# Interleaving the high and low parts of every second unit's stationary operand in a decoder step

## The chip, the cores and the metric

The kernel runs on one core of one Trainium2 chip. The metric is device microseconds of one execution. Shown are three runs, of which the median counts, and one more execution that was profiled.

## The reference

The reference is one step of a one-layer decoder: a prompt of 2048 tokens and 32 sample tokens share the weights. After the mixer come cross-attention and a gated feed-forward block, with a norm around each. Nearly all of the arithmetic is in products of activations and weights:

```
m = concat(o_gla, y) @ w_out            # h = x + norm(m)
a = softmax((hn @ w_xq) . mk) . mv @ w_xo   # h = h + norm(a)
f = (silu(hf @ w_gate) * (hf @ w_up)) @ w_down   # h = h + norm(f)
```

All inputs are float32, and the model width is 1024, the hidden width 2816.

## The kernel before, in words

The mixer comes first (to about 850 us). The rest is one long list of passes, each a set of matrix products, and this list is what the change touches. The passes are o (output projection of the mixer), s (scores of the cross-attention), v (its values), g0, g1, g2 (gate and up projections of three blocks of tokens) and d0, d1, d2 (three parts of the sum of the down projection, over 3, 4 and 4 units of the hidden width).

A pass is worked unit by unit. In o, s, v and d a unit is one of 8 groups `j` of 256 tokens; in g it is one of 11 slices `u` of the hidden width, once for the gate and once for the up projection (`m`), so 22 units. Within a unit a block product of 2 by 2 is formed with seven products in place of eight, which `TURN` lists; the sums and differences of blocks that this takes are made on DVE (line 1650). The seven are called parts here. A part is `nt` tiles of 128 rows (3 in d0, 4 elsewhere), and each tile is three matmuls.

Three, because each float32 operand is split into a high part, rounded to the matmul's float32r, and a low part, the rest. `three` (lines 133 to 137) adds high by high, high by low, low by high: lines 135 and 136 load the high stationary part, 137 the low one. The moving operand (tiles `r` and `e`, with 512, 384 or 272 columns) is held through the pass. The stationary operand, 128 by 128 at a time, comes from the tile `s` of class `Unit`: 1024 words on each partition, 4 buffers. `Unit.hi` copies the block as float32r into `s` on ACT (line 1668), and the function that it returns puts the block minus that copy into `s` on DVE (line 1670). The high words lie in words 0 to 511 and the low ones in 512 to 1023, each tile's 128 columns next to each other. Both are made four parts ahead of the matmuls that use them (`ahead_ = 4`); the load of the next raw units is issued with part 6. The matmuls accumulate in four PSUM banks (`accA` twice, `accB`, `accC`), which ACT and DVE empty after each part.

The order of the work is written out by hand: the list `order`, and what is done between parts (pieces of the moving operand, evacuations, sample tokens, norms of finished rows), is recorded in program order on every engine.

Of the kernel before, what the change touches and what calls it, by code (L numbers as in the profile page):

```python
# [20 lines left out]
P = 128  # L21
# [16 lines left out]
def f(ap):  # L38
    return ap.bitcast(F32)
# [3 lines left out]
def hymba_kernel(ctx: ExitStack, tc: tile.TileContext, a: dict, o: dict, dbg: dict | None = None):  # L43
# [49 lines left out]
    mixT = tc.dram_tile([NJ, P, 2048], F32, name="mixT")  # L93
# [39 lines left out]
    def three(ps, wh, wl, ah, al, start, stop, more=False):  # L133

        nc.tensor.matmul(ps, lhsT=wh, rhs=ah, start=start, stop=False, skip_group_check=more)  # L135
        nc.tensor.matmul(ps, lhsT=wh, rhs=al, start=False, stop=False, skip_group_check=more)  # L136
        nc.tensor.matmul(ps, lhsT=wl, rhs=ah, start=False, stop=stop, skip_group_check=more)  # L137
# [1394 lines left out]
    xq = tc.dram_tile([NJ, P, 2048], F32, name="xq")  # L1532
    pT = tc.dram_tile([NJ, P, 2048], F32, name="pT")
# [103 lines left out]
    class Unit:  # L1637

        def __init__(self, src, n):
            self.w = n * P
            self.q = src(praw.tile([P, 2048], F32, name="raw", bufs=2))
            self.t, self.got = {}, {}

# [6 lines left out]
        def hi(self, i):  # L1652

            if i == 1:
                self.op("S1", 2, 3, ALU.add)
            if i == 3:
                self.op("S2", "S1", 0, ALU.subtract)
            if i == 2:
                self.op("S4", 1, "S2", ALU.subtract)
            if i == 5:  # L1660
                self.op("S3", 0, 2, ALU.subtract)
            v = {0: self.q[0], 1: self.q[1], 6: self.q[3]}
            v = v[i] if i in v else self.t[{3: "S1", 2: "S2", 5: "S4", 4: "S3"}[i]]
            w = self.w
            s = pf.tile([P, 1024], F32R, name="s", bufs=4)
            hi, lo = s[:, 0:w], s[:, 512:512 + w]
            h3, l3 = (x.rearrange("p (k c) -> p k c", c=P) for x in (hi, lo))
            nc.scalar.activation(h3, v, AF.Copy)  # L1668
            self.got[i] = hi, lo
            return lambda: nc.vector.tensor_tensor(l3, v, f(h3), op=ALU.subtract)  # L1670

    def unit_x(src, j):

        def load(raw):
            nc.sync.dma_start(out=raw, in_=src[j])
            v = raw.rearrange("p (h u e t) -> p h u e t", h=2, e=2, t=P)
            return [v[:, i // 2, :, i % 2] for i in range(4)]
        return Unit(load, 4)

    def unit_g(u, m):  # L1680
        def load(raw):
            nc.sync.dma_start(out=raw, in_=a["w_gu"][m, u].rearrange("p q c -> p (q c)"))
            return [raw[:, i * 512:(i + 1) * 512].rearrange("p (k c) -> p k c", c=P) for i in range(4)]
        return Unit(load, 4)

    def unit_d(p, j):
        u0, n = PARTS[p]

        def load(raw):
            r = raw[:, 0:n * 512]  # L1690
            nc.sync.dma_start(out=r, in_=aT[j][:, u0:u0 + n].rearrange("p u c -> p (u c)"))
            v = r.rearrange("p (u e h t) -> p u e h t", e=2, h=2, t=P)
            return [v[:, :, i % 2, i // 2] for i in range(4)]
        return Unit(load, n)

# [441 lines left out]
    units = {}  # L2139

    def load_unit(n):
        if n < len(work):
            k, g, _ = work[n]
            kind, i, _ = passes[k]
            units[n] = unit_g(*g) if kind == "g" else unit_d(i, g) if kind == "d" else unit_x({"o": mixT, "s": xq, "v": pT}[kind], g)

    def enter(k):

        nonlocal pg, pd
        kind, i, _ = passes[k]  # L2150
        rate[:] = RATES[kind]
        if kind == "o":
            gain_row(px, "ln_mix_post")
            for u in range(4):
                aux.append(weight_sums(lambda n, u=u: flat2(wqk)[n, u], wX[1], u))
        if kind == "s":
            for u in range(4):
                aux.append(weight_sums(lambda n, u=u: flat2(wvo)[n, u], wX[2], u))
        if kind == "v":
            gain_row(px, "ln_xa_post")  # L2160
        if kind == "g":
            if i == 0:
                rctx.close()
                pg = fctx.enter_context(tc.tile_pool(name="pg", bufs=1, reuse_waits="tile"))

                pg.tile([P, 1536], F32, name="og")
            for u in range(NU):
                if u % (len(BLOCKS) - 1) == i:
                    aux.append(weight_sums(lambda n, u=u: a["w_down"][n, u], wT, u))
            if i + 1 == len(BLOCKS):  # L2170
                aux.append(samples_down())
        if kind == "d" and i == 0:
            fctx.close()
            pd = ctx.enter_context(tc.tile_pool(name="pd", bufs=1, reuse_waits="tile"))
            pd.tile([P, D], F32, name="m")
            pd.tile([P, D], F32, name="ga")
# [40 lines left out]
    lo = [None]  # L2217
# [46 lines left out]
    evs, banks, held, ys = {}, {}, {}, {}  # L2264
# [7 lines left out]
    for e, (n, i) in enumerate(order):  # L2272
        k, g, left = work[n]
        kind, b, gs = passes[k]
        if i == 0:
            cur = n
            if begins[n]:
                if coming:
                    now, coming = coming, None
                enter(k)  # L2280
            held[n] = now
            w = now.w
            if kind == "g":
                if g[1] == 0:
                    sg = {}
                evs[n] = evac_gate(sg, w) if g[1] == 0 else evac_up(sg, w, b, g[0])
            elif kind == "d":
                h = {}
                if n + 1 == len(work):
                    for m in range(2):  # L2290
                        h[m] = stage()
                        nc.sync.dma_start(out=h[m], in_=hX[rows(g, m)])
                top = n in ys
                y = ys.pop(n, {})
                stays = left == 1 and b + 1 < len(PARTS)
                if stays:
                    ys[n + 1] = y
                evs[n] = evac_d(b, g, y, h, top, stays)
            else:
                evs[n] = quads(g, *{"o": (after_mix, True), "s": (after_scores, False), "v": (after_values, True)}[kind])  # L2300
            if left == 2 and k + 1 < len(passes):
                before_loads(k)
                coming = pieces_of(k + 1)
        if i == 2 and n + 1 < len(work) and on_top(n + 1):

            ys[n + 1] = {}
            for m in range(2):
                ys[n + 1][m] = pd.tile([P, D], F32, name="y", bufs=6)
                nc.sync.dma_start(out=ys[n + 1][m], in_=yp[work[n + 1][1]][:, m * D:(m + 1) * D])

        nt = PARTS[b][1] if kind == "d" else 4
        w = held[n].w
        if i == 0:
            banks[n, "A"] = accA.tile([P, 512], F32, name="accA")
        if i == 1:
            banks[n, "B"] = accB.tile([P, 512], F32, name="accB")
        if i == 3:
            banks[n, "C"] = accC.tile([P, 512], F32, name="accC")
        ps = banks[n, {1: "B", 3: "C", 5: "C"}.get(i, "A")]
        while i not in held[n].full:  # L2320
            held[n].step()
        sh, sl = units[n].got[i]
        start = i in (0, 1, 3)
        for kt in range(nt):
            ks = slice(kt * P, (kt + 1) * P)
            three(ps[:, 0:w], sh[:, ks], sl[:, ks], *held[n].moving(i, kt), start and kt == 0, kt == nt - 1, not start)
        if left == 1:
            spent.add((k, i))
        evs[n](NAMES[i], ps)

        todo, later[:] = list(later), []
        for fn in todo:
            fn()
        part(e + ahead_)

        p = coming if work[cur][2] == 1 else now if begins[cur] else None
        if p:
            p.larger()
        tick()
        if p:  # L2340
            p.smaller()
        if kind == "d" or not coming and now.done() and (k != XG or samp2):
            due[1] += rate[1]
            while due[1] >= 10:
                due[1] -= 10
                step(aux)
        pin()
        due[0] += rate[0]
        while due[0] >= 10:
            due[0] -= 10  # L2350
            step(back)
        pin(True)
        if samp2 is None and k == XG and not posts:
            leave_attention()
# [99 lines left out]
```

## Time and profile before

| what | value |
|---|---|
| median of 3 runs | 2815.03 us (2814.23 to 2822.64) |
| the profiled execution | 2820.75 us |
| its span, first to last instruction | 2819.0 us |
| PE busy / weight loads busy | 97% / 84% |
| DVE / ACT / POOL busy | 74% / 52% / 19% |
| matmuls in all / in the nine passes | 15207 / 9408 |
| start of pass o, end of pass d2 | 850.8 us, 2809.0 us |

In the profile PE is the matmul and PEld the weight load, which runs while the matmul before it streams. A matmul's own duration contains its way through the array, and several are under way at once, so the time that a matmul costs is read from the distance between starts, not from its duration. The same holds for weight loads.

### The profile page before, as it was taken

To read this page: it belongs to the slowest core of one execution; us is meant where nothing else is said; L and a number is where in the kernel's file an instruction comes from. 1 tells how busy PE (TensorE), PEld (TensorE's weight loads), DVE (VectorE), ACT (ScalarE), POOL (GpSimd) and SP (SyncE) were. 2 spreads that over 40 slices of the span, in tenths; PEclk is the share of its full clock that TensorE was granted. 3 is DMA by queue.
4 is the path that set the end of the run, shared out by engine and by line. 5 is a ranking of instruction groups with operands and counts; after the bars stand their busy time and mean duration, and the time that the engine had idled before them with its cause. 6 is when DMAs were issued, how large, how long until landed. Compare 5 with 4: busy or idle time off the path is not lost.

```text
span 2819.0 us, 41809 instructions
## 1 busy us (share of the span) xinstructions
PE 2729.5 (97%) x15207; PEld 2367.6 (84%) x15207; DVE 2079.1 (74%) x3831; ACT 1472.8 (52%) x2921; POOL 536.8 (19%) x722
## 2 busy tenths in 40 slices
PE   8999999999998999999899999999999999999998
PEld 8987888788886878878799888899998998788786
DVE  7676677776757787677888787667678878574776
ACT  5545554554546787777755434434445555353432
POOL 2142332321321321015321210001000001000011
PEclk9999999999999999999999999999999999999999
DMA  7345435343266785468864567775234436464765
GB/s 255 113 142 188 148 106 160 118 131 90 83 215 226 282 291 223 146 189 254 263 222 179 177 237 243 253 254 178 98 137 171 156 120 209 168 219 99 239 152 132
DMA packets 151102, 512.17 MB, mean 182 GB/s; under 512 B 18176, under 2 KB 29488, under 8 KB 137328
## 3 DMA queue, kind: packets, MB, share of 16 engines
q1 hardware_dynamic: 94560, 331.81, 36.0%
q0 software_dynamic: 44240, 152.82, 16.8%
q10 hardware_dynamic: 12096, 24.86, 2.7%
q8 instruction: 120, 1.97, 0.3%
q14 instruction: 86, 0.70, 0.1%
HBM read 365.76 MB, written 143.67 MB: 181 GB/s over the span
## 4 chain that ended last, share of the span: by engine, by line
PE 75%; DVE 13%; ACT 5%; DMA 3%; issue 3%; POOL 1%; DVEq 0%; ACTq 0%; SPq 0%; POOLq 0%
PE accA L135 9%; PE accA L136 9%; PE accA L137 9%; PE accC L135 5%; PE accC L136 5%; PE accC L137 5%; PE acc L135 5%; PE acc L136 5%; PE acc L137 5%; PE accB L135 2%; PE accB L137 2%; PE accB L136 2%; DVE s L1670 2%; DVE sum L1650 2%; ACT r L1739 1%
## 5 line engine op out<-in xcount | busy, mean ns | idle before, releaser
L135 PE MATMUL accA<-r,s 128*128 128x512 f32 (+2 forms) x1792 | 637.2, 356 | 19.0 <-ACT r L1739 7.2
L137 PE MATMUL accA<-r,s 128*128 128x512 f32 (+2 forms) x1792 | 629.1, 351 | 2.9 <-DVE s L1670 2.8
L136 PE MATMUL accA<-r,s 128*128 128x384 f32 (+2 forms) x1472 | 502.7, 342 | 2.4 <-DVE r L1743 2.4
L135 PEld LDWEIGHTS accA<-r,s 128*128 128x128 f32 x1792 | 339.2, 189 | 70.9 <-ACT r L1739 11.0
L1668 ACT ACTIVATE s<-sum 128x512 fp32r<-128x512 f32 (+1 forms) x456 | 282.5, 620 | 218.9 <-DVE sum L1650 105.0
L137 PEld LDWEIGHTS accA<-r,s 128*128 128x128 f32 x1792 | 339.7, 190 | 33.2 <-DVE s L1670 4.0
L135 PE MATMUL accC<-r,s 128*128 128x512 f32 (+2 forms) x896 | 318.8, 356 | 9.2 <-ACT s L1668 3.2
L1670 DVE TENSOR_TENSOR s<-sum,s 128x512 fp32r<-128x512 f32 (+1 forms) x456 | 306.8, 679 | 20.1 <-ACT s L1668 19.8
L137 PE MATMUL accC<-r,s 128*128 128x512 f32 (+2 forms) x896 | 314.3, 351 | 0.0
L136 PEld LDWEIGHTS accA<-r,s 128*128 128x128 f32 x1472 | 279.0, 190 | 19.2 <-DVE r L1743 3.6
L1670 DVE TENSOR_TENSOR s<-raw,s 128x512 fp32r<-128x512 f32 (+1 forms) x342 | 233.7, 683 | 52.0 <-ACT s L1668 50.9
L136 PE MATMUL accC<-r,s 128*128 128x384 f32 (+2 forms) x736 | 251.3, 341 | 0.5 <-DVE r L1743 0.5
L1668 ACT ACTIVATE s<-raw 128x512 fp32r<-128x512 f32 (+1 forms) x342 | 213.3, 624 | 72.1 <-PE accC L137 49.8
L129 ACT ACTIVATE whi<-wraw 128x1024 fp32r<-128x1024 f32 (+2 forms) x140 | 128.9, 934 | 184.2 <-PE acc L136 104.5
L135 PEld LDWEIGHTS accC<-r,s 128*128 128x128 f32 x896 | 169.8, 189 | 37.2 <-ACT s L1668 7.8
L130 DVE TENSOR_TENSOR wlo<-wraw,whi 128x1024 fp32r<-128x1024 f32 (+2 forms) x140 | 156.2, 1127 | 48.0 <-ACT whi L129 47.3
L137 PEld LDWEIGHTS accC<-r,s 128*128 128x128 f32 x896 | 169.7, 189 | 14.9 <-DVE s L1670 0.2
L143 POOL TENSOR_TENSOR rs<-ms,nhalf 128x1 f32<-128x1 f32 (+4 forms) x125 | 111.0, 889 | 360.3 <-DVE ms L141 343.9
L135 PE MATMUL acc<-xhl,whi 128*128 128x512 f32 (+1 forms) x464 | 168.1, 363 | 8.3 <-ACT xhl L294 8.2
L137 PE MATMUL acc<-xhl,wlo 128*128 128x512 f32 (+1 forms) x464 | 164.3, 355 | 1.7 <-DVE wlo L130 1.7
L136 PE MATMUL acc<-xhl,whi 128*128 128x512 f32 (+1 forms) x464 | 164.1, 355 | 0.2 <-DVE xhl L295 0.2
L1650 DVE TENSOR_TENSOR sum<-raw 128x512 f32<-128x512 f32 (+1 forms) x228 | 156.4, 686 | 3.6
(696 smaller groups left out, 5857.9 us busy)
## 6 DMA issues: line engine op xcount, KB each, us to landing
raw<-in_w_gu_dram SPq DMA_DIRECT2D x66, 1024.0 KB, 4.9
wraw<-in_w_in_fm_dram SPq DMA_DIRECT2D x52, 512.0 KB, 3.6
wraw<-in_w_in_tm_dram SPq DMA_DIRECT2D x48, 512.0 KB, 3.9
st<-in_w_down_dram SPq DMA_DIRECT2D x37, 512.0 KB, 6.2
aT<-og POOLq DMA_DIRECT2D x22, 768.0 KB, 4.6
raw<-aT SPq DMA_DIRECT2D x16, 1024.0 KB, 6.3
out_y_dram<-y POOLq DMA_DIRECT2D x28, 512.0 KB, 6.1
yp<-y POOLq DMA_DIRECT2D x28, 512.0 KB, 6.6
```

What stands on the lines that cost most here:

```text
L129: last[0] = nc.scalar.activation(hi[:, cs], raw[:, cs], AF.Copy)
L130: nc.vector.tensor_tensor(lo[:, cs], raw[:, cs], f(hi)[:, cs], op=ALU.subtract)
L135: nc.tensor.matmul(ps, lhsT=wh, rhs=ah, start=start, stop=False, skip_group_check=more)
L136: nc.tensor.matmul(ps, lhsT=wh, rhs=al, start=False, stop=False, skip_group_check=more)
L137: nc.tensor.matmul(ps, lhsT=wl, rhs=ah, start=False, stop=stop, skip_group_check=more)
L143: nc.gpsimd.tensor_tensor(out=rs[:rows, :cols], in0=ms[:rows, :cols], in1=nhalf[:rows, :cols], op=ALU.pow)
L1650: nc.vector.tensor_tensor(t[out], x, y, op=o)
L1668: nc.scalar.activation(h3, v, AF.Copy)
L1670: return lambda: nc.vector.tensor_tensor(l3, v, f(h3), op=ALU.subtract)
L1739: nc.scalar.activation(hi, v, AF.Copy)
```

## The change

The stationary tile `s` keeps its size and its four buffers. What changes is where the words lie in it.

- In every odd unit (odd `j`, or odd `u`) the high and low words are interleaved. At a step of 2, which passes o, v, g0, g2 and d1 take, the high word of a column lies beside its low word, and columns are two words apart. At a step of 8, which s, g1 and d2 take, the eight words of one column (four tiles, high and low) lie side by side, and the columns of a tile are eight words (32 bytes) apart. Even units stay as they were.
- In d0, which has 384 words of each part, both parts stay contiguous and begin 16 words (64 bytes) later for each `j`.

So 224 of the 798 splits write at a step of 2 and 126 at a step of 8, and of the 9408 matmuls of the passes 2688 and 1512 load such weights (a third of each in every line of `three`). The arithmetic, the number of instructions, their order on every engine and their waits stay the same; the lines of `Unit.hi` become 1672 (ACT) and 1674 (DVE). The core of the diff:

```
-        def __init__(self, src, n):
-            self.w = n * P
+        def __init__(self, src, n, turn=1, shift=0):
+            self.w, self.turn, self.shift = n * P, turn, shift
...
             s = pf.tile([P, 1024], F32R, name="s", bufs=4)
-            hi, lo = s[:, 0:w], s[:, 512:512 + w]
-            h3, l3 = (x.rearrange("p (k c) -> p k c", c=P) for x in (hi, lo))
+            if self.turn == 2:
+                h3, l3 = (s[:, 0:2 * w].rearrange("p (k c z) -> p z k c", z=2, c=P)[:, z] for z in range(2))
+            elif self.turn == 8:
+                h3, l3 = (s.rearrange("p (c k z) -> p z k c", z=2, c=P)[:, z] for z in range(2))
+            else:
+                h3, l3 = (s[:, at:at + w].rearrange("p (k c) -> p k c", c=P) for at in (self.shift, 512 + self.shift))
             nc.scalar.activation(h3, v, AF.Copy)
...
-        return Unit(load, n)
+        return Unit(load, n, (1, 2, 8)[p] if j % 2 else 1, 0 if p else 16 * j)
...
-            units[n] = unit_g(*g) if kind == "g" else unit_d(i, g) if kind == "d" else unit_x({"o": mixT, "s": xq, "v": pT}[kind], g)
+            units[n] = unit_g(*g, (2, 8, 2)[i] if g[0] % 2 else 1) if kind == "g" else unit_d(i, g) if kind == "d" else unit_x({"o": mixT, "s": xq, "v": pT}[kind], g, {"o": 2, "s": 8, "v": 2}[kind] if g % 2 else 1)
...
-            ks = slice(kt * P, (kt + 1) * P)
-            three(ps[:, 0:w], sh[:, ks], sl[:, ks], *held[n].moving(i, kt), start and kt == 0, kt == nt - 1, not start)
+            three(ps[:, 0:w], sh[:, kt], sl[:, kt], *held[n].moving(i, kt), start and kt == 0, kt == nt - 1, not start)
```

More of the change, by code (lines that the diff above doesn't have):

```diff
@@ L1665, in hi, with unit_x @@
             s = pf.tile([P, 1024], F32R, name="s", bufs=4)
-            hi, lo = s[:, 0:w], s[:, 512:512 + w]
-            h3, l3 = (x.rearrange("p (k c) -> p k c", c=P) for x in (hi, lo))
+            if self.turn == 2:
[4 more added lines that the diff above has]
+                h3, l3 = (s[:, at:at + w].rearrange("p (k c) -> p k c", c=P) for at in (self.shift, 512 + self.shift))
             nc.scalar.activation(h3, v, AF.Copy)
-            self.got[i] = hi, lo
+            self.got[i] = h3, l3
             return lambda: nc.vector.tensor_tensor(l3, v, f(h3), op=ALU.subtract)
-    def unit_x(src, j):
+    def unit_x(src, j, turn):
         def load(raw):
@@ L1677, in load, with unit_g @@
             return [v[:, i // 2, :, i % 2] for i in range(4)]
-        return Unit(load, 4)
-    def unit_g(u, m):
+        return Unit(load, 4, turn)
+    def unit_g(u, m, turn):
         def load(raw):
@@ L1683, in load @@
             return [raw[:, i * 512:(i + 1) * 512].rearrange("p (k c) -> p k c", c=P) for i in range(4)]
-        return Unit(load, 4)
+        return Unit(load, 4, turn)
     def unit_d(p, j):
```

## The prediction

> **What bounds the kernel now.** I read the page first, then a table by pass, the waits of one pass, and single instructions for the distance between starts. The page shows an engine that hardly rests, and a chain of work that lies mostly on it:
>
> ```profile
> span 2819.0 us, 41809 instructions
> PE 2729.5 (97%) x15207; PEld 2367.6 (84%) x15207; DVE 2079.1 (74%) x3831; ACT 1472.8 (52%) x2921; POOL 536.8 (19%) x722
> PE 75%; DVE 13%; ACT 5%; DMA 3%; issue 3%; POOL 1%; DVEq 0%; ACTq 0%; SPq 0%; POOLq 0%
> PE accA L135 9%; PE accA L136 9%; PE accA L137 9%; PE accC L135 5%; PE accC L136 5%; PE accC L137 5%; PE acc L135 5%; PE acc L136 5%; PE acc L137 5%; PE accB L135 2%; PE accB L137 2%; PE accB L136 2%; DVE s L1670 2%; DVE sum L1650 2%; ACT r L1739 1%
> ```
>
> DVE's split (line 1670) holds 2% of the span on that chain, which I need below. The table by pass says what room each engine has in each stage. Its columns are the stretch, its length, and busy time and count of PE, PEld, DVE, ACT and POOL; the rows are o, s, v, g0, g1, g2, d0, d1, d2.
>
> ```profile
> 850.80:1034.20 183.40, 173.88 (x778) 139.68 (x776) 141.62 (x230) 126.86 (x258) 48.12 (x72) 0.96 0.76 260
> 1034.20:1206.20 172.00, 169.03 (x812) 139.88 (x810) 128.93 (x213) 128.07 (x297) 24.45 (x40) 1.00 0.57 204
> 1206.20:1380.30 174.10, 168.42 (x786) 138.37 (x785) 135.19 (x234) 129.17 (x295) 67.17 (x93) 0.99 0.78 240
> 1380.30:1758.40 378.10, 366.51 (x2208) 340.63 (x2206) 311.05 (x631) 189.93 (x368) 65.45 (x98) 0.99 0.61 210
> 1758.40:2108.90 350.50, 346.30 (x2113) 328.36 (x2109) 251.40 (x431) 155.54 (x295) 25.07 (x41) 1.00 0.53 184
> 2108.90:2367.90 259.00, 246.44 (x1881) 237.86 (x1882) 213.74 (x410) 138.69 (x279) 12.36 (x14) 0.99 0.45 158
> 2367.90:2494.30 126.40, 125.13 (x561) 95.63 (x561) 79.07 (x134) 56.30 (x104) 14.48 (x20) 0.99 0.59 204
> 2494.30:2648.60 154.30, 153.01 (x673) 125.79 (x673) 93.76 (x136) 62.73 (x97) 11.38 (x14) 1.00 0.61 162
> 2648.60:2809.00 160.40, 155.26 (x673) 126.87 (x672) 121.71 (x198) 59.25 (x122) 20.71 (x29) 0.99 0.64 163
> ```
>
> In every pass PE is busy nearly all the time, at a granted clock close to 1. Where PE does wait, it is for little; these are all its waits in g1:
>
> ```profile
> PE mx L1429 <- DMA sraw<-in_cache_k_dram: 3.0, 1, 3.0
> PE accA L135 <- ACT s L1668: 0.6, 1, 0.6
> PE mx L1429 <- DVE sqm L1425: 0.5, 1, 0.5
> ```
>
> So no gain can come from waits; it would have to come from the pace of the matmuls. That pace is the distance between starts. First and last of twelve matmuls, with 384 columns (g1), 512 (d1) and 272 (g2):
>
> ```profile
> 1801.65 0.33 PE L135 MATMUL accB<-r,s 128*128 128x384 f32 x1
> ...
> 1803.56 0.34 PE L137 MATMUL accB<-r,s 128*128 128x384 f32 x1
> ...
> 2599.64 0.39 PE L135 MATMUL accA<-r,s 128*128 128x512 f32 x1
> ...
> 2602.14 0.39 PE L137 MATMUL accA<-r,s 128*128 128x512 f32 x1
> ...
> 2199.75 0.29 PE L135 MATMUL accC<-r,s 128*128 128x272 f32 x1
> ...
> 2201.13 0.29 PE L137 MATMUL accC<-r,s 128*128 128x272 f32 x1
> ```
>
> Over eleven distances these are 1.91, 2.50 and 1.38 us, so 173.6, 227.3 and 125.5 ns a matmul. From 384 to 512 columns it grows by 53.7 ns, 0.42 ns a column; 512 columns are then 215 ns, and some 12 ns come on top at every width. The moving stream sets the pace, and a weight load hides behind it. How long it needs by itself shows where two loads follow each other with the array free:
>
> ```profile
> 1804.83 0.19 PEld L135 LDWEIGHTS accC<-r,s 128*128 128x128 f32 x1 [0.41 <-issue]
> 1804.94 0.19 PEld L136 LDWEIGHTS accC<-r,s 128*128 128x128 f32 x1
> ```
>
> The second begins 0.11 us after the first. The cover over a load is thus 117 ns at 512 columns, 64 ns at 384 and 16 ns at 272. A load may grow by a factor of 2.07, 1.58 or 1.14 before the matmuls feel it.
>
> **The change part by part.** It removes and moves nothing: every engine and queue has the same instructions in the same order with the same waits. Three kinds of instruction meet the new layout: the weight load reads at a step, ACT writes at a step, DVE reads one input and writes at a step.
>
> No row of the trace shows a weight load at a step, so I bound it. The nearest rows are small vector operations; the first reads both inputs at a step of 128 words, the second reads adjacent words, and the next two are the same function on ACT, from 16 words at a step of 4 and from 64 adjacent words:
>
> ```profile
> L673 DVE TENSOR_TENSOR el<-bd x4: 165/178/180, 113.9 to 715.1; 128x8 f32<-128x8 f32 x4
> ...
> L2005 DVE TENSOR_TENSOR s_f<-t,sg x33: 163/168/171, 2132.2 to 2365.9; 128x16 f32<-128x16 f32 x33
> ...
> L1250 ACT ACTIVATE gebl<-gb x1: 217/217/217, 1586.4 to 1586.4; 128x16 f32<-128x16 f32 x1
> ...
> L1249 ACT ACTIVATE ge<-gb 128x64 f32<-128x64 f32 x1 | 0.3, 258 | 0.0
> L1668 ACT ACTIVATE s<-sum 128x512 fp32r<-128x512 f32 x424 | 265.7, 627 | 194.5 <-DVE sum L1650 100.3 <-PE accA L137 41.8 <-PE accB L137 29.1
> L1670 DVE TENSOR_TENSOR s<-sum,s 128x512 fp32r<-128x512 f32 x424 | 288.5, 686 | 17.3 <-ACT s L1668 16.9
> ```
>
> DVE grows by (686 - 168)/496 = 1.04 ns for each adjacent word, so 8 adjacent words would take 168 - 8 x 1.04 = 160 ns. The row with a step took 178: 18 ns more, 2.2 ns a word for two stepped inputs, 1.1 for each. ACT's slope from 64 to 512 words is (627 - 258)/448 = 0.82 ns; 16 adjacent words would be 258 - 48 x 0.82 = 219, and the stepped row took 217: no cost.
>
> *Weight load at a step of 8 (s, g1, d2).* Lower bound, as ACT's row: none, 0.11 us. Upper bound, as DVE's: 128 x 1.1 = 141 ns more, 0.25 us. I take a doubling, 0.22 us, nearer to DVE's end, since the steps of DVE's row (128 words) and of this load both leave no neighbour near, while ACT's row has a step half as long. Below the bound of none I see nothing: adjacent words already take 0.86 ns each, twice the moving column's 0.42, and words further apart give no reason to be faster. At 0.22 us the load shows where the stream is shorter: in g1, 0.22 - 0.1736 = 46.4 ns. g1 has 5 odd slices of 11, each with 2 units of 7 parts of 12 matmuls: 840 matmuls, 39 us. In s and d2 the stream has 227.3 ns and still covers it, by 7 ns, for 672 matmuls. Without that cover, at 0.25 us, these cost 672 x 23 ns = 15 us and g1 840 x 76 ns = 64 us.
>
> *Weight load at a step of 2 (o, v, g0, g2, d1).* Bounds as above; I take ACT's row, no cost, since it did not slow at four words, a wider step. The page "SBUF — State Buffer" of the Trainium skill (SBUF: two separate sides) has lines of 16 bytes, at full rate with two hits on a line: a step of 2 words would be free and one of 8 not, as I have it. But by it ACT's row, one hit a line, should have paid too, and it did not; for a weight load no run here shows either.
>
> *DVE's split at a step of 8.* Between nothing and 512 x 2.2 = 1.1 us more on 0.69. I take one stepped stream, 0.56 us, because reading and writing use separate operands that can overlap. 126 splits give 71 us of DVE work. In s (28 of them) DVE goes from 129 to 145 of 172 us, in g1 (70) from 251 to 291 of 350 and in d2 (28) from 122 to 138 of 160. That still fits, and the parts are made four ahead (10.9 us at 512 columns), which hides a late one. Behind a longer split on DVE's queue stand the sums of the next part and the evacuation of a bank, for which PE waits. What leaks through I price by the chain: 2% of 2819 us is 56 us, 82 of the 798 splits at 0.69 us, a tenth. A tenth of 71 us is 7 us; in g1, where PE itself gets slower, I count nothing, which leaves 3 us. *At a step of 2* I take nothing, as for the load; *ACT's copy* costs nothing by its row (a read, where the copy writes), and with 0.42 us more on 350 copies it would still have room (its fullest pass is s, 128 of 172 us).
>
> *The start 64 bytes later in d0*: contiguous words stay contiguous. Nothing, either way.
>
> A rule that speaks against the step of 2: "Vector Engine (DVE) Microarchitecture Reference" of the Trainium skill (Measured stream behaviour on trn2) has full rate only for runs of at least two adjacent words, and 1.7 to 2.5 ns a word otherwise. An estimate by it: 350 splits, each 0.3 to 0.7 us longer, 105 to 245 us of DVE work, a tenth of which, 10 to 25 us, would take the place of my 3. The row of DVE at a step of 128 agrees that distance costs; no row shows two words.
>
> The sum: 39 + 3 = 42 us. Against the profiled execution (2820.75 us, its span and 1.75 us around it) that is 2863; that execution lies 5.7 us above the median of the runs, so beside the median I expect 2815 + 42 = 2857 us.
>
> **The rivals.**
> *No cost (other side; not slower).* The mechanism is the cover: a weight load has 64 ns to spare in g1, and if a stepped load grows by less than a factor of 1.58 the matmuls keep 173.6 ns. For it: ACT's row, and that a contiguous load needs 0.86 ns a word where the moving operand arrives at 0.42, so a path with room exists. Against it: DVE's row. Time: 2815 + 3, at most 2820 us. The page "TensorE: Matmul & The Clock Gate" of the Trainium skill (LDWEIGHTS) counts columns alone for a load, which by itself gives this result; the 0.11 us agree with 128 columns, but no row has a step.
> *DVE alone.* The loads cost nothing, but a split at a step of 8 takes 1.1 us more: 139 us of work. DVE would stand at 93 to 95% in s, g1 and d2, and a tenth on the chain makes 14 us: 2829. Against it: the depth of four parts.
> *The step of 2 costs as the step of 8 does.* Then g0 pays 39 us too, and g2, with the least cover, 840 x (220 - 125.5) ns = 79 us: 2857 + 118 = 2975. Against it: ACT's row.
> *Faster.* The 12 ns that each matmul takes beyond its stream could come from a load and a stream meeting at the same place in memory. If another layout avoided that in the 4200 odd matmuls, 50 us would go: 2765. Against it: the 12 ns are about the same at all three widths, while the load meets the stream at different places.
>
> **How the numbers follow.** Chances: forecast 0.36, no cost 0.33, DVE alone 0.12, step of 2 as well 0.10, faster 0.09. The likeliest gives 2857 us; its own range, from a load that shows only half as much (20 us) to the upper bound (64 + 15 + 6 = 85), is 2835 to 2900. The whole range takes in no cost with a run's scatter, 2806, and ends at 2900; it leaves out the two last cases, 0.19. A measurement of this kernel can tell about 0.3%, 8 us, from no change. Faster by more: 0.09. Within: 0.33. Slower by more: 0.36 + 0.12 + 0.10 = 0.58.
>
> **What would show it.** Right: in odd units of g1 the starts are 0.22 us apart and in even ones 0.174; g0, g2 and all passes with 512 columns keep their pace; g1 is 39 us longer; line 1674 at 128x4x128 takes about 1.25 us. Wrong: starts of 0.174 us in all of g1 (no cost), 0.25 or more in s and d2 (a larger factor), a changed pace in odd units of g0 or g2 (the step of 2 counts), or PE waits on DVE that make up the difference.

## The result, and the profile after

The changed kernel takes 2896.56 us (median of 4 runs, 2894.18 to 2898.09) beside 2814.63 us for the one before: ratio 1.0286, 95% interval 1.0273 to 1.0299. That is 82 us, twice the 42 of the forecast and just inside the range, which ends at 2900.

The table by pass of the changed kernel, rows and columns as before (o, s, v, g0, g1, g2, d0, d1, d2):

```profile
850.90:1035.40 184.50, 174.26 (x779) 140.48 (x777) 141.79 (x230) 127.81 (x259) 48.13 (x72) 0.97 0.75 259
1035.40:1215.60 180.20, 178.05 (x810) 161.16 (x809) 141.40 (x211) 141.87 (x295) 24.88 (x40) 0.98 0.54 194
1215.60:1392.20 176.60, 170.90 (x787) 141.08 (x786) 136.58 (x236) 130.55 (x295) 67.28 (x93) 0.99 0.77 234
1392.20:1768.60 376.40, 364.84 (x2208) 339.51 (x2206) 309.21 (x631) 193.17 (x368) 64.27 (x98) 0.99 0.62 212
1768.60:2178.30 409.70, 405.53 (x2112) 387.74 (x2109) 287.08 (x431) 196.03 (x295) 25.32 (x41) 1.00 0.45 158
2178.30:2436.00 257.70, 246.89 (x1880) 238.16 (x1881) 213.74 (x410) 141.65 (x280) 12.35 (x14) 0.98 0.45 159
2436.00:2564.60 128.60, 127.39 (x562) 95.99 (x562) 79.20 (x134) 56.41 (x104) 14.63 (x20) 0.99 0.58 202
2564.60:2720.60 156.00, 155.13 (x674) 127.81 (x673) 94.14 (x137) 63.61 (x97) 11.38 (x14) 1.00 0.60 161
2720.60:2886.70 166.10, 161.58 (x673) 146.05 (x671) 135.44 (x197) 75.05 (x122) 20.71 (x29) 0.99 0.60 156
```

The three passes with a step of 8 grew: g1 from 350.5 to 409.7 us (59.2), s by 8.2, d2 by 5.7. The other six moved by -1.7 to +2.5, 4.5 in sum, o, v, d0 and d1 up and g0 and g2 down. Together these are 77.6 us, beside 77.4 between the spans (2896.4 and 2819.0). That is less than 82 because the profiled execution of the kernel before lay 6 us above the median of its runs, and this one 1.5. PE stays busy throughout, and its waits in g1 are fewer than before, none of them on a split:

```profile
PE mx L1429 <- DMA sraw<-in_cache_k_dram: 2.9, 1, 2.9
PE mx L1429 <- DVE sqm L1425: 0.5, 1, 0.5
```

So PE was slowed without waiting. The starts in g1 show how. First and last of twelve matmuls of an even unit, then of an odd one; and two weight loads of that odd unit:

```profile
1939.68 0.33 PE L135 MATMUL accA<-r,s 128*128 128x384 f32 x1
...
1941.58 0.34 PE L137 MATMUL accA<-r,s 128*128 128x384 f32 x1
...
1975.39 0.41 PE L135 MATMUL accA<-r,s 128*128 128x384 f32 x1
...
1978.06 0.41 PE L137 MATMUL accA<-r,s 128*128 128x384 f32 x1
```

```profile
1975.20 0.34 PEld L135 LDWEIGHTS accA<-r,s 128*128 128x128 f32 x1
1975.44 0.34 PEld L136 LDWEIGHTS accA<-r,s 128*128 128x128 f32 x1
```

Even units keep 1.90/11 = 173 ns. Odd ones take 2.67/11 = 243 ns, and the weight loads, 0.34 us long where they were 0.19, start 0.24 us apart: the matmuls now go at the pace of the loads. 840 matmuls at 69 ns more are 58 us, nearly all of what g1 gained.

At a step of 2 with 512 columns (odd unit of d1) there is a small change that the forecast didn't have:

```profile
2654.47 0.39 PE L135 MATMUL accC<-r,s 128*128 128x512 f32 x1
...
2657.03 0.39 PE L137 MATMUL accC<-r,s 128*128 128x512 f32 x1
```

2.56/11 = 233 ns in place of 227. The splits at a step of 8 are longer on both engines. First DVE's and then ACT's splits in g1, 154 of each, before and after:

```profile
1758.40:2108.90 350.50, 104.64 (x154) 1.00 0.53 184
...
1768.60:2178.30 409.70, 140.29 (x154) 1.00 0.45 158
```

```profile
1758.40:2108.90 350.50, 96.98 (x154) 1.00 0.53 184
...
1768.60:2178.30 409.70, 138.33 (x154) 1.00 0.45 158
```

70 of the splits are at the step, so each of these takes 0.51 us more on DVE and 0.59 on ACT. In g0, where 70 are at a step of 2, DVE's 153 splits take 105.97 us, before 105.51: no more. ACT's 154 take 100.14 us there, before 96.94, which is 0.05 us more for each at the step.

### The profile page after: what moved, and what is told of

Same layout as the page of the kernel before. It is cut to its first block, busy times and chain, and to the rows that moved or that the text cites. A ratio compares the mean times of both kernels' runs of the same rounds, so it can differ in the third digit from the quotient of the medians.

```text
span 2896.4 us, 41809 instructions
## 1 busy us (share of the span) xinstructions
PE 2809.6 (97%) x15207; PEld 2472.2 (85%) x15207; DVE 2140.7 (74%) x3831; ACT 1552.4 (54%) x2921; POOL 535.6 (18%) x722
## 4 chain that ended last, share of the span: by engine, by line
PE 68%; issue 11%; DVE 11%; ACT 4%; DMA 3%; POOL 2%; DVEq 0%; POOLq 0%; SPq 0%; ACTq 0%
PE accA L135 8%; PE accA L136 8%; PE accA L137 8%; PE acc L135 5%; PE acc L136 5%; PE acc L137 5%; PE accC L135 5%; PE accC L136 4%; PE accC L137 4%; PE accB L135 2%; PE accB L137 2%; PE accB L136 2%; DVE s L1674 2%; DVE sum L1650 1%; ACT r L1743 1%
## 5 line engine op out<-in xcount | busy, mean ns | idle before, releaser
L135 PE MATMUL accA<-r,s 128*128 128x512 f32 (+2 forms) x1792 | 654.3, 365 | 17.5 <-ACT r L1743 6.3
L137 PE MATMUL accA<-r,s 128*128 128x512 f32 (+2 forms) x1792 | 643.8, 359 | 3.6 <-DVE s L1674 3.5
L136 PE MATMUL accA<-r,s 128*128 128x384 f32 (+2 forms) x1472 | 517.3, 351 | 2.3 <-DVE r L1747 2.3
L1672 ACT ACTIVATE s<-sum 128x512 fp32r<-128x512 f32 (+1 forms) x456 | 331.6, 727 | 221.6 <-DVE sum L1650 107.6
L135 PEld LDWEIGHTS accA<-r,s 128*128 128x128 f32 x1792 | 385.3, 215 | 64.1 <-ACT r L1743 10.8
L137 PEld LDWEIGHTS accA<-r,s 128*128 128x128 f32 x1792 | 385.7, 215 | 29.7 <-DVE s L1674 4.8
L1674 DVE TENSOR_TENSOR s<-sum,s 128x512 fp32r<-128x512 f32 (+1 forms) x456 | 344.1, 762 | 22.1 <-ACT s L1672 21.8
L135 PE MATMUL accC<-r,s 128*128 128x512 f32 (+2 forms) x896 | 327.8, 366 | 8.1 <-ACT sg L1981 3.1
L136 PEld LDWEIGHTS accA<-r,s 128*128 128x128 f32 x1472 | 315.6, 214 | 17.6 <-DVE r L1747 3.8
L137 PE MATMUL accC<-r,s 128*128 128x512 f32 (+2 forms) x896 | 322.3, 360 | 0.0
L1674 DVE TENSOR_TENSOR s<-raw,s 128x512 fp32r<-128x512 f32 (+1 forms) x342 | 262.4, 767 | 57.3 <-ACT s L1672 56.6
L1672 ACT ACTIVATE s<-raw 128x512 fp32r<-128x512 f32 (+1 forms) x342 | 249.0, 729 | 68.3 <-PE accC L137 49.7
L136 PE MATMUL accC<-r,s 128*128 128x384 f32 (+2 forms) x736 | 258.6, 351 | 0.4 <-DVE r L1747 0.4
L135 PEld LDWEIGHTS accC<-r,s 128*128 128x128 f32 x896 | 192.8, 215 | 33.8 <-ACT sg L1981 6.9
L137 PEld LDWEIGHTS accC<-r,s 128*128 128x128 f32 x896 | 193.1, 215 | 12.6 <-DVE s L1674 0.2
L136 PEld LDWEIGHTS accC<-r,s 128*128 128x128 f32 x736 | 157.6, 214 | 8.4 <-DVE r L1747 1.4
```

## The experiments

The theory after the result: a weight load whose words lie 8 apart takes 0.243 us by itself, and shows wherever the stream of the matmul is shorter. Rivals: the scattered writes of ACT and DVE hold PE up, by the memory or by lateness; or interleaving costs in itself.

**Only the reads at a step of 8.** The splits stay contiguous; the matmuls of odd units in s, g1 and d2 take their words at the step, and so read other words than were meant. The step of 2 and the shift are left out, here and in the next two runs.

```
-            self.got[i] = h3, l3
+            self.got[i] = (h3, l3) if self.turn == 1 else [s.rearrange("p (c k z) -> p z k c", z=2, c=P)[:, z] for z in range(2)]
```

> The splits write contiguous words as before; only the matmuls of the odd units of s, g1 and d2 take their stationary words at a step of 8 (so they read other words of the tile, high and low mixed, and the result differs). If the weight load at a step of 8 is the cost (theory): starts 0.243 us apart in odd units of g1 and 0.245 in s and d2, splits at 0.63 and 0.68 us, g1 +59 us, s and d2 together +14, total 2885 to 2892. If the slow writes of ACT and DVE hold PE up (rival): starts as before, total 2812 to 2822.

Measured: 2888.61 us, ratio 1.0254 (1.0239 to 1.0269). Twelve matmuls in an odd unit of g1, and a split of that unit:

```profile
1968.05 0.41 PE L135 MATMUL accA<-r,s 128*128 128x384 f32 x1
...
1970.71 0.41 PE L137 MATMUL accA<-r,s 128*128 128x384 f32 x1
```

```profile
1965.81 0.68 DVE L1669 TENSOR_TENSOR s<-sum,s 128x512 fp32r<-128x512 f32 x1
```

The pace is 2.66/11 = 242 ns while the split takes its old 0.68 us. Nearly the whole loss, 73 us of 82, is there with contiguous writes, as the theory had it.

**Only the writes at a step of 8.** The other half; again the matmuls of these units read other words than were meant.

```
             h3, l3 = (s[:, at:at + w].rearrange("p (k c) -> p k c", c=P) for at in (0, 512))
+            self.got[i] = h3, l3
+            if self.turn == 8:
+                h3, l3 = (s.rearrange("p (c k z) -> p z k c", z=2, c=P)[:, z] for z in range(2))
             nc.scalar.activation(h3, v, AF.Copy)
```

> The other half: the splits of the odd units of s, g1 and d2 write at a step of 8, and the matmuls take contiguous words (again other words, so the result differs). Theory: splits take 1.2 us on both engines, starts stay at 0.173 and 0.227 us, and the lookahead hides the rest, total 2813 to 2824. Rival (the writes are the cost): total 2870 to 2895.

Measured: 2824.19 us, ratio 1.0031 (1.0021 to 1.0042). A split, two ends of twelve matmuls, and g1 in the table by pass:

```profile
1940.28 1.24 DVE L1671 TENSOR_TENSOR s<-sum,s 128x512 fp32r<-128x512 f32 x1
```

```profile
1939.38 0.34 PE L135 MATMUL accA<-r,s 128*128 128x384 f32 x1
...
1941.30 0.34 PE L137 MATMUL accA<-r,s 128*128 128x384 f32 x1
```

```profile
1757.30:2113.00 355.70, 348.25 (x2112) 327.79 (x2108) 286.15 (x431) 194.46 (x295) 25.57 (x41) 1.00 0.52 181
```

While a split of 1.24 us runs, the matmuls keep 1.92/11 = 174 ns: scattered writes don't slow the reads of PE. What is lost is 9 us by the medians, just over the upper edge of what the theory gave. Of the 6.0 us between the profiled executions (spans 2825.0 and 2819.0) 5.2 lie in g1, where PE is busy 2 us longer and idle 3 us longer. Its waits there come to 6.8 us in place of 4.1, and 1.5 of these are on splits, in place of 0.6. So lateness costs something where the loads don't slow PE; where the rest of the 9 us lies the trace does not show.

**A step of 4.** As the change, with 4 words where it has 8, contiguous elsewhere.

```
+            if self.turn == 4:
+                h3, l3 = (s.rearrange("p (a c b z) -> p z a b c", a=2, b=2, z=2, c=P)[:, z] for z in range(2))
```

> As the change, but a step of 4 words (16 bytes) where it has 8, and contiguous where it has 2 or the shift. If a load pays for every word that has no neighbour within 16 bytes, as at a step of 8: load 0.33 us, total 2885 to 2892, splits 1.2 us. If the price grows with the distance: load between 0.19 and 0.33 us, total 2815 to 2880. If four words are as free as the small ACT row of the prediction had it: total 2812 to 2820, splits 0.63 and 0.68 us.

Measured: 2876.84 us, ratio 1.0214 (1.0198 to 1.0229). An odd unit of g1:

```profile
1964.82 0.40 PE L135 MATMUL accC<-r,s 128*128 128x384 f32 x1
...
1967.39 0.40 PE L137 MATMUL accC<-r,s 128*128 128x384 f32 x1
```

2.57/11 = 234 ns, 9 less than at a step of 8. Four words apart are not free, though the small ACT row had suggested it, but nearly as dear as eight, and a load is 0.33 us long, as the first expectation had it. The total lies 8 us below that expectation, though, and inside the range of the second, a price that grows with the distance. The total alone can't decide between them; the map of steps below does. The splits are dearer at this step too: those of g1 take 133.69 us on DVE and 132.41 on ACT, 0.42 and 0.51 us more for each of the 70.

**Steps of 2 and 8 exchanged.** The sharpest test of a load time of its own, since it moves the step of 8 to the pass with the shortest stream.

```
-        return Unit(load, n, (1, 2, 8)[p] if j % 2 else 1, 0 if p else 16 * j)
+        return Unit(load, n, (1, 8, 2)[p] if j % 2 else 1, 0 if p else 16 * j)
...
-            units[n] = unit_g(*g, (2, 8, 2)[i] if g[0] % 2 else 1) ... {"o": 2, "s": 8, "v": 2}[kind] if g % 2 else 1)
+            units[n] = unit_g(*g, (8, 2, 8)[i] if g[0] % 2 else 1) ... {"o": 8, "s": 2, "v": 8}[kind] if g % 2 else 1)
```

> The steps of 2 and 8 change places: 8 in o, v, g0, g2 and d1, 2 in s, g1 and d2, shift in d0 as in the change. If a load has a time of its own of 0.243 us and shows only beyond the stream: g0 +59 us, g2 840 x (0.243 - 0.126) = +98, o, v and d1 +17, s and d2 +4, g1 none, total 2990 to 3000. If the matmul is slowed by a factor (1.40 in g1): g2 gets 840 x 0.050 = +42 and the total is 2930 to 2945.

Measured: 2992.91 us, ratio 1.0627 (1.0610 to 1.0645), inside the theory's numbers and 48 us above the rival's. g0, g1 and g2 by pass, and twelve matmuls of g2 with 272 columns:

```profile
1400.30:1827.20 426.90, 421.35 (x2208) 398.51 (x2206) 343.30 (x631) 230.35 (x368) 64.79 (x98) 1.00 0.54 185
1827.20:2179.60 352.40, 347.82 (x2113) 329.02 (x2109) 251.70 (x431) 158.50 (x295) 25.07 (x41) 0.99 0.53 183
2179.60:2531.70 352.10, 341.94 (x1881) 335.71 (x1882) 249.22 (x410) 180.09 (x279) 12.36 (x14) 0.99 0.33 116
```

```profile
2344.47 0.41 PE L135 MATMUL accA<-r,s 128*128 128x272 f32 x1
...
2347.13 0.41 PE L137 MATMUL accA<-r,s 128*128 128x272 f32 x1
```

g1 is back at 352 us, g2 went from 259 to 352, and its odd matmuls stand at 2.66/11 = 242 ns, the same as with 384 columns. The time belongs to the load, not to the matmul. That the total came out as expected is partly luck, though. g0 gained 49 us for 59 expected, while PE's idle time there shrank from 11.6 to 5.5 us; g2 gained 93 for 98; o, v and d1 gained 28 for 17. At 244 to 245 ns the 1008 odd matmuls of these three make 18, and the runs don't explain the other 10.

**A map of steps.** Contiguous splits; in g1 and g2 the odd units read at steps of 3 to 7, two even ones at a step of 2: u = 4 with the high words from an even and the low ones from an odd word, u = 6 the other way round. These units read other words than were meant, as in the first experiment.

```
+    STEPS = {1: 3, 3: 4, 5: 5, 7: 6, 9: 7, 4: 2, 6: -2}
...
+                self.got[i] = [[s[:, at:at + P * st].rearrange("p (c q) -> p c q", q=st)[:, :, 0] for at in (2 * k + z + odd for k in range(4))] for z in range(2)]
```

> A map: splits contiguous as before; in g1 and g2 the matmuls of unit u take stationary words at a step of 3 (u=1), 4 (3), 5 (5), 6 (7) and 7 (9), at a step of 2 from an even word (4) and from an odd word (6), else 1; the result differs. If a load is priced by new lines of 16 bytes: step 3 between (3 of 4 words begin a line), 4 to 7 all alike at 0.243 us in both passes, step 2 free from either start. If distance counts: the start-to-start time grows from step 3 to step 7. If only neighbours count (runs of two words): all steps from 2 up cost in g2, where 0.126 us hides least.

One run, 2928.91 us. Twelve matmuls of g2 at a step of 3, 4, 2 (u = 4), 5 and 7:

```profile
2180.90 0.34 PE L135 MATMUL accA<-r,s 128*128 128x272 f32 x1
...
2182.85 0.34 PE L137 MATMUL accA<-r,s 128*128 128x272 f32 x1
...
2235.09 0.40 PE L135 MATMUL accA<-r,s 128*128 128x272 f32 x1
...
2237.67 0.39 PE L137 MATMUL accA<-r,s 128*128 128x272 f32 x1
...
2271.77 0.28 PE L135 MATMUL accA<-r,s 128*128 128x272 f32 x1
...
2273.16 0.29 PE L137 MATMUL accA<-r,s 128*128 128x272 f32 x1
...
2296.64 0.39 PE L135 MATMUL accA<-r,s 128*128 128x272 f32 x1
...
2299.14 0.40 PE L137 MATMUL accA<-r,s 128*128 128x272 f32 x1
...
2422.25 0.40 PE L135 MATMUL accC<-r,s 128*128 128x272 f32 x1
...
2424.82 0.40 PE L137 MATMUL accC<-r,s 128*128 128x272 f32 x1
```

177, 235, 126, 227 and 234 ns. By their medians the unit at a step of 6 stands at 228 ns and the other one at a step of 2 at 127. In g1 the medians are 178, 233, 229, 231 and 237 ns for steps of 3 to 7, so there too the load sets the pace. A step of 2 stays free (126 is the stream's own pace; in g1 it took 176 ns for 173), 3 costs a part, 4 and more cost nearly alike and do not rise with distance. Steps of 4 to 7 lie 6 to 17 ns below the 243 that was expected of them. This fits a price by groups of four words: at 4 every word opens a new group, 235/128 = 1.84 ns each; at 3 three words in four do, 96 x 1.84 = 176; at 2 half of them, 118, which hides under 126. At 1 it would be 59 ns, and the load takes 110, so there something else sets its time. "SBUF — State Buffer" of the Trainium skill (SBUF: two separate sides) has such lines of 16 bytes, and the loads here agree with it. That 5 and 6 are a little below 4, and 8 a little above, it doesn't say, and the runs don't explain it.

**A map of starts in d0.** Everything contiguous, the start moved by 0, 4, 8, 16, 32, 64, 96, 128 words for j = 0 to 7.

```
-        return Unit(load, n, (1, 2, 8)[p] if j % 2 else 1, 0 if p else 16 * j)
+        return Unit(load, n, 1, 0 if p else (0, 4, 8, 16, 32, 64, 96, 128)[j])
```

> All units contiguous; in d0 both parts begin 0, 4, 8, 16, 32, 64, 96 and 128 words later for j = 0 to 7. If the extra 3 to 6 ns in d0 of the change come from where the load starts relative to a period of 64 words (256 bytes): 0.227 us for j = 0, 5 and 7, 0.230 to 0.234 for the others. If it comes from the shift itself, all but j = 0 are at 0.230 or more. If it was chance, all are at 0.227.

One run, 2816.06 us. Nine matmuls at the start of word 0 and of word 8:

```profile
2371.33 0.39 PE L135 MATMUL accA<-r,s 128*128 128x512 f32 x1
...
2373.15 0.39 PE L137 MATMUL accA<-r,s 128*128 128x512 f32 x1
...
2404.14 0.40 PE L135 MATMUL accA<-r,s 128*128 128x512 f32 x1
...
2406.01 0.40 PE L137 MATMUL accA<-r,s 128*128 128x512 f32 x1
```

1.82/8 = 227.5 and 1.87/8 = 233.8 ns. By medians over whole units: 227, 227, 233, 236, 232, 227, 232 and 227 ns for the eight starts. 64 and 128 words are as 0 and 96 as 32, which fits a period of 64 words (256 bytes); 4 words don't matter. The fit is not exact: in the changed kernel, starts of 48 and 112 words stand at 230 and 233 ns.

**The step of 2 alone, and the shift alone** (the diff of the change with 1 in place of 8 and no shift; with 1 everywhere and the shift).

> Only the step of 2 (o, v, g0, g2, d1), no step of 8 and no shift. Theory: 0.233 in place of 0.227 us in the odd units of o, v and d1, 1008 x 6 ns = 6 us, g0 and g2 as before, total 2817 to 2823, ratio 1.001 to 1.003. Rival (interleaving costs in itself, by the writes): 2830 or more. If it helps in g2 (0.125 for 0.127): down to 2814.

> Only the shift in d0. Theory: d0 0.230 to 0.233 us in most units, 441 matmuls x 4 ns, +2 us, ratio 1.0005 to 1.0012. Rival: no change that shows.

Measured: 2820.94 us, ratio 1.0019 (1.0010 to 1.0028), and 2816.17 us, ratio 1.0007 (0.9998 to 1.0016). The step of 2 costs about 5 us, all in passes with 512 columns: in its trace o, v and d1 are 2.0, 2.0 and 2.6 us longer, no other pass more than 0.1. The shift can't be told from no change by its time; in its trace d0 is 128.5 us long beside 126.5, as in the changed kernel.

The parts add up: 1.0254, 1.0031, 1.0019 and 1.0007 are 0.0311 over one, beside 0.0286 for all together. That the sum is a little larger would fit the trace, where PE in g1 waits for no split once the loads slow it; but each interval reaches 0.001 or more to either side, so the difference can be noise. No layout tried is faster than the one before.

## Why the prediction was right or wrong

- *The mechanism, that a load at a step of 8 outgrows the stream in g1, was right.* It shows in the odd units alone and moves with the step (first and fourth experiment). The rival of no cost falls with the 243 ns there.
- *"I take a doubling, 0.22 us" is the step that was mis-sized.* A load takes 0.243 us, a factor of 2.2. The upper bound from DVE's row of eight words, 0.25 us, was nearly exact and its 64 us for g1 close to the 59 measured; the choice below it cost 20 us in g1.
- *"in s and d2 the stream ... still covers it, by 7 ns"* failed for the same reason: 0.243 us is over 227 ns, the pace there is 244 to 245, and the two passes grew by 14 us, 12 of them by 672 matmuls at 17 to 18 ns more, where the bound without cover had 15. A cover of 7 ns under a guess of +-30 was none.
- *A step of 2 at no cost* was right for the load (g0 and g2 kept their pace) and so the rival that priced it like a step of 8 falls. With 512 columns 6 ns a matmul came on top, 5 us in all, which no row had shown.
- *DVE's split*: 0.56 us were expected, 0.51 measured. With PE unslowed the leak was 9 us, where the tenth gave 7. In the changed kernel s, g1 and d2 gained 73 us, of which the paces of their matmuls make 58 and 12; the other 3 are what the forecast had, but a pass that a run leaves unchanged differs by as much between runs. DVE alone, as a rival, falls: its 14 us were to be the whole, and the loads make most of the loss.
- *ACT's copy "costs nothing by its row"* was wrong: 0.59 us more. It was hidden, as the alternative beside it said. At a step of 2, 0.05 us more. The row was of 16 words, where a cost of 1 ns a word hides in the scatter (two operations of one form on ACT, 8 words at one step, lines 671 and 672, take 220 and 202 ns), and a read where the copy writes.
- *The start 64 bytes later, "nothing"*: d0 grew by 2 us, below what a timing can tell.
- *A rule against the step of 2* ("Vector Engine (DVE) Microarchitecture Reference" of the Trainium skill, Measured stream behaviour on trn2) is not borne out here: the 153 splits of DVE in g0, 70 of them at a step of 2, took 105.97 us, and 105.51 when all were contiguous.
- *Faster*: the 12 ns beyond the stream did not go in any layout.

## What to carry to other kernels

A weight load is hidden only while it is shorter than the stream of the matmul before it: compare the two as distances between starts, pass by pass, and take the narrowest pass as the price. Here a stationary tile could be interleaved at a step of two float32 words for at most 6 ns a matmul; from four words on each load here took more than twice its time, whatever the step. Where a cost is bounded by two rows of a trace, and the cover lies between the bounds, say so and count the cover as open.

## What the runs showed of the hardware

Matmuls with 512 columns run at 227 to 236 ns, depending on where the stationary operand starts within 64 words of memory, and at 233 ns when its columns are two words apart; those with 384 columns stayed at 173 ns at a step of 2 in the changed kernel, and took 176 in the map of steps. Why was not tried.

ACT and DVE both pay about 1 ns for each word written at a step of 8 (0.59 and 0.51 us on 512 words), though DVE reads a stepped operand as well, and beside such writes the matmuls of g1 kept their 174 ns.
